# Norms by matmul, denominators kept in SBUF, a new chunk order and operand loads by threes in a hybrid encoder layer

## The chip, the cores and the metric

The kernel runs on one core of a Trainium2 chip. The metric is the device time of one execution in microseconds. Three runs of the kernel before took 1853.64, 1854.88 and 1856.46 us; the median, 1854.88 us, is the time that the change is compared with.

## The reference, cut to what matters

One encoder layer is applied to a prompt of 1024 tokens and to a sample of 512 tokens with the same weights. Model width is 1024, the FFN's hidden width 2816, everything in float32.

```
h    = rms_norm(x) * (1 + sc1) + sh1
proj = h @ w_in                       # q, k, v of 12 heads; u, v of 4 gMLP groups
o_g, lse_g = dilated_window_attention(q, k, v) for 3 groups of 4 heads
wts  = softmax(lse over the 3 groups)
mix  = concat(wts_g * o_g, u * (W_s LN(v) + b)) @ w_out
x    = x + gt1 * rms_norm(mix)
h    = rms_norm(x) * (1 + sc2) + sh2
f    = (silu(gate) * up) @ w_down,  gate, up = split(h @ w_gu)
y    = x + gt2 * rms_norm(f)
```

The weighting of the three attention groups by their log-sum-exps is done in the kernel as one division: the unnormalised outputs of the groups are multiplied by the reciprocal of the sum of their denominators. A head's slot (0 or 1) says which half of the four heads of a group it belongs to, and each slot has its own denominators.

## The kernel before, in words

The activations lie with features on the 128 partitions, in chunks of 128 features by 512 tokens, eight chunks for the model width (`KC`). The prompt is two halves of 512 tokens (group 0 and group 1, together the class `P`), the sample is group 2 (class `S`). Every product is done as three matmuls of float32r operands, high by high, high by low and low by high (`mm3`, L160). For that, `split` (L139) makes the high part of an operand with a cast on ACT (L140) and the low part with a subtraction on DVE or POOL (L141). Weights come from DRAM by one DMA queue that SP issues in order (four raw buffers `wraw`), are split, and are used from `whl`; chunks come through `load_chunk` (L237) into three buffers `xc`.

The stages are: input projections and attention of the sample and then the prompt, gMLP of the two prompt halves, out-projections of groups 2, 0 and 1 (`out_proj`, `post`), the FFN of the sample (`ffn`, `down`), and the FFN of the prompt, whose first product over both halves is a Winograd product with seven products instead of eight (`operands` writes 28 operand chunks to `ops` in DRAM, `operands_in` loads and splits them, `ffn_up` multiplies), and last `ffn_down` for the halves 0 and 1.

Work that is not the matmuls of the running stage is written as generators. They are queued in `self.back`, and each product calls `tick`, which lets them go on; `alongside` starts one beside the running stage. After that a scheduling pass orders the instructions of each engine, so that the order on an engine is not that of the code.

The places that the change touches: `attention_slot` (L713) takes the reciprocal of a slot's denominators (L729) and writes them to `rden` in DRAM (L731); `mix_in` (L902) loads each of the eight chunks of the attention and gMLP output, loads the denominators again for each of the six attention chunks, multiplies (L907) and splits with the low part on POOL. `post` (L831) evacuates an out-projection tile into an `sc` buffer (L843), squares it (L844), and when the norm is there multiplies by it (L856), adds the residual (L857) and stores. The norm is either `rms` (L202: a matmul with ones sums over the partitions, POOL takes the power, ACT makes a diagonal tile and matmuls with ones spread it over the partitions) or, after the FFN of groups 2 and 0, `rms_slow` (L195):

```
self.nc.gpsimd.partition_all_reduce(ss, ss, channels=128, reduce_op=RED.add)
y = self.t("rs", [128, 512])
self.rsqrt(y, self.t2("tb"), self.t2("tb"), ss, 1.0 / D, RMS_EPS)
```

where `rsqrt` (L170) is twelve DVE operations on 128x512 tiles, nine of them in the loop L179 to L181, with two of the two `tb` buffers. `ffn_up` makes the combined weights on DVE (L929, L986), and evacuates products into `tb` on ACT (L1036).

Of the kernel before, what the change touches and what calls it, by code (L numbers as in the profile page):

```python
# [10 lines left out]
F32R = mybir.dt.float32r  # L11
I32 = mybir.dt.int32
# [7 lines left out]
D = 1024  # L20
KC = 8
# [9 lines left out]
RSQRT_MAGIC = 0x5F3759DF  # L31
# [47 lines left out]
class Layer:  # L79
    def __init__(self, tc, ctx, a):  # L80
# [16 lines left out]
        self.rs2 = {}  # L97
        self.pending = []
# [71 lines left out]
    def rsqrt(self, y, v, t, ss, scale, eps):  # L170

        nc = self.nc
        nc.vector.tensor_scalar(out=v, in0=ss, scalar1=scale, scalar2=eps, op0=ALU.mult, op1=ALU.add)
        nc.vector.tensor_scalar(out=y.bitcast(I32), in0=v.bitcast(I32), scalar1=1, scalar2=None,
                                op0=ALU.arith_shift_right)
        nc.vector.tensor_scalar(out=y.bitcast(I32), in0=y.bitcast(I32), scalar1=-1, scalar2=RSQRT_MAGIC,
                                op0=ALU.mult, op1=ALU.add)
        for _ in range(3):
            nc.vector.tensor_tensor(out=t, in0=y, in1=y, op=ALU.mult)  # L179
            nc.vector.scalar_tensor_tensor(out=t, in0=v, scalar=-0.5, in1=t, op0=ALU.mult, op1=ALU.mult)  # L180
            nc.vector.scalar_tensor_tensor(out=y, in0=t, scalar=1.5, in1=y, op0=ALU.add, op1=ALU.mult)  # L181

# [11 lines left out]

    def rms_slow(self, ss):  # L195

        self.nc.gpsimd.partition_all_reduce(ss, ss, channels=128, reduce_op=RED.add)  # L197
        y = self.t("rs", [128, 512])
        self.rsqrt(y, self.t2("tb"), self.t2("tb"), ss, 1.0 / D, RMS_EPS)
        return y  # L200
# [512 lines left out]
    def attention_slot(self, grp, sp, steps, between=None, start=None):  # L713
# [9 lines left out]
        def behind():  # L723
            while len(vs) < 3:
                yield
            yield from weave(self.softmax(grp, sc[0]), self.softmax(grp, sc[1]))
            den = self.t4("st")
            yield from self.values(grp, sp, sc, vs, den)
            self.nc.vector.reciprocal(out=den[:, :grp.n], in_=den[:, :grp.n])  # L729
            for hf, gi in enumerate(grp.halves):  # L730
                self.nc.sync.dma_start(out=self.rden[gi, sp], in_=den[:, 512 * hf:512 * hf + 512])  # L731
            yield
# [98 lines left out]
    def post(self, gi, product, G, xsrc, dst, follow, steps):  # L831
# [32 lines left out]
        def behind():  # L864
            rs = self.rms(ss) if follow else self.rms_slow(ss)
# [36 lines left out]
    def mix_in(self, gi, hs, kcs=range(KC), tags=("h",) * KC):  # L902
        for kc in kcs:
            x = self.load_chunk(self.mix[gi, kc])
            if kc < 6:
                r = self.load_chunk(self.rden[gi, kc % 2])
                self.nc.vector.tensor_tensor(out=x, in0=x, in1=r, op=ALU.mult)  # L907
            h = self.t(tags[kc], [128, 2, 512], F32R)
            self.split(h[:, 0], h[:, 1], x, self.nc.gpsimd)
            hs.append(h)  # L910
            yield

    def out_proj(self, gi, hs, steps):
        def product(mt):
            w = self.weights(self.a["wout"][mt], share=SHARE[3])
            ps = self.p("mm")
            self.mm3(ps, w, range(KC), hs)
# [46 lines left out]
    def operands_in(self, ops, os):  # L964
        for o in os:
            for k in range(4):
                x = self.load_chunk(self.ops[o, k])
                h = self.t(self.OPS[4 * o + k], [128, 2, 512], F32R)
                self.split(h[:, 0], h[:, 1], x)
                ops[o].append(h)  # L970
                yield
# [101 lines left out]
    def ffn(self, gi, h2, ops):  # L1073
# [19 lines left out]
        self.back.append(self.operands_in(ops, range(2)))  # L1093
# [23 lines left out]
    def run(self):  # L1117
# [55 lines left out]
        self.back.append(self.mix_in(0, hs[0]))  # L1173
# [8 lines left out]
        self.back.insert(0, self.ffn_in(2, h2))  # L1182
# [10 lines left out]
        for _ in self.operands_in(ops, range(2, 7)):  # L1193
            pass
# [10 lines left out]
STEPS = (3, 6, 3, 4)  # L1205
H0 = 'V'
H1 = 'V'
H2 = 'V'
H3 = 'P'
# [60 lines left out]
```

## Time and profile before

| what | value |
|---|---|
| median of three runs | 1854.88 us (1853.64 to 1856.46) |
| the profiled execution's own time | 1856.45 us |
| span of its records | 1854.7 us |
| mean granted clock of TensorE | 0.986 |
| TensorE (PE) busy | 1785.3 us, 96% |
| VectorE (DVE) busy | 1049.6 us, 57% |
| ScalarE (ACT) busy | 694.3 us, 37% |
| GpSimd (POOL) busy | 113.3 us, 6% |

Busy time counts instructions that run, not those that wait. The span is the time from the first record to the last of one execution; its own time lies 1.75 us above it. Where the stages lie in the span: the first out-projection tile is evacuated (L843) at 574.6 us, the first tile of the sample's FFN (L1086) at 759.0 us, the first and the last product of the Winograd FFN (L1036) at 1146.5 and 1571.4 us; what comes after are the down products of the prompt.

### The profile page before, as it was taken

What the parts mean: (1) busy time and instruction counts of PE and PEld (TensorE: products, weight loads), DVE (VectorE), ACT (ScalarE), POOL (GpSimd) and SP (SyncE); (2) the same over time, 40 slices, a digit from 0 to 9 for tenths busy, and PEclk for the clock granted to TensorE, in tenths of its full rate; (3) what the DMA queues carried; (4) which work ended last, traced back from release to release, by engine and by line L of the source; (5) the groups of instructions that cost most, each with busy time, mean ns of one, the idle gap of its engine ahead of it and who ended that gap; (6) DMA issues with size and microseconds to landing.
All of it is one profiled execution on the core that took longest, in us unless ns stands there. A gap on an engine that the chain in (4) does not pass through costs nothing.

```text
span 1854.7 us, 22895 instructions
## 1 busy us (share of the span) xinstructions
PE 1785.3 (96%) x8442; PEld 1402.8 (76%) x8442; DVE 1049.6 (57%) x1675; ACT 694.3 (37%) x1196; POOL 113.3 (6%) x70
## 2 busy tenths in 40 slices
PE   6999999999999889899999998799999999999997
PEld 3787777766787667677888886588888888888886
DVE  4686625524876556766444325766666576623733
ACT  4653511411355346444333324233232233533322
POOL 0010100300121132000000000000000000000001
PEclk9999999999999999899999998899999999999998
DMA  8424312211243465568422435332222222734632
GB/s 323 148 95 161 130 63 98 80 68 63 93 144 114 146 215 194 185 233 299 143 94 94 135 97 161 112 123 80 92 80 86 80 91 73 238 98 157 216 106 77
DMA packets 133617, 245.05 MB, mean 132 GB/s; under 512 B 14976, under 2 KB 20352, under 8 KB 133504
## 3 DMA queue, kind: packets, MB, share of 16 engines
q1 hardware_dynamic: 133360, 243.51, 39.5%
q8 instruction: 66, 1.08, 0.2%
q14 instruction: 47, 0.39, 0.1%
q10 hardware_dynamic: 144, 0.07, 0.0%
HBM read 204.20 MB, written 39.32 MB: 131 GB/s over the span
## 4 chain that ended last, share of the span: by engine, by line
PE 84%; issue 5%; DVE 5%; DMA 3%; ACT 1%; POOL 1%; SPq 0%; DVEq 0%; ACTq 0%; POOLq 0%
PE pmm L158 69%; PE ppv L158 9%; PE pst L158 6%; DMA xc<-rden 1%; DVE sc L618 1%; POOL st L653 1%; DMA xc<-ops 1%; DVE whl L141 1%; DMA xc<-in_x 0%; DVE sc L856 0%; DMA h<-in_wada 0%; POOL h L141 0%; DMA xc<-mix 0%; DVE sd L618 0%; ACT tb L389 0%
## 5 line engine op out<-in xcount | busy, mean ns | idle before, releaser
L158 PE MATMUL pmm<-h,whl 128*128 128x512 f32 x4008 | 990.4, 401 | 32.6 <-ACT whl L140 11.2
L158 PEld LDWEIGHTS pmm<-h,whl 128*128 128x128 f32 x4008 | 749.8, 190 | 241.6 <-issue 28.7
L141 DVE TENSOR_TENSOR whl<-wraw,whl 128x512 fp32r<-128x512 f32 (+1 forms) x420 | 290.4, 695 | 317.7 <-ACT whl L140 317.6
L140 ACT CAST whl<-wraw 128x512 fp32r<-128x512 f32 (+1 forms) x420 | 253.2, 606 | 469.7 <-PE pmm L158 342.6
L158 PE MATMUL pmm<-qk,whl 128*128 128x512 f32 (+1 forms) x570 | 141.1, 394 | 0.0
L158 PEld LDWEIGHTS pmm<-qk,whl 128*128 128x128 f32 x570 | 107.1, 188 | 25.3 <-DVE whl L141 0.3
L158 PE MATMUL pmm<-v,whl 128*128 128x512 f32 x405 | 102.6, 398 | 10.7 <-ACT tb L1036 10.7
L158 PE MATMUL pmm<-h,sc 128*128 128x512 f32 x408 | 101.0, 395 | 0.0
L158 PEld LDWEIGHTS pmm<-v,whl 128*128 128x128 f32 x405 | 77.5, 192 | 28.6 <-ACT tb L1036 11.1
L158 PEld LDWEIGHTS pmm<-h,sc 128*128 128x128 f32 x408 | 76.7, 188 | 18.3
L158 PE MATMUL pst<-qk 64*128 64x128 f32 (+3 forms) x384 | 66.9, 319 | 0.9 <-DVE qk L141 0.9
L140 ACT CAST whl<-sd 128x512 fp32r<-128x512 f32 x53 | 32.9, 620 | 87.9 <-PE ppv L158 69.1
L158 PE MATMUL ppv<-h,whl 128*128 128x512 f32 x264 | 65.1, 395 | 0.0
L158 PEld LDWEIGHTS pst<-qk 64*128 64x128 f32 (+1 forms) x384 | 49.2, 187 | 20.6 <-issue 12.9
L197 POOL PARTITION_ALL_REDUCE acc<-acc x2 | 7.0, 3514 | 895.7 <-issue 568.8
L158 PEld LDWEIGHTS ppv<-h,whl 128*128 128x128 f32 x264 | 49.6, 188 | 11.9
L140 ACT CAST h<-xc 128x512 fp32r<-128x512 f32 x56 | 34.5, 621 | 54.7 <-DVE xc L907 29.9
L653 POOL PARTITION_ALL_REDUCE st<-st x8 | 34.6, 4326 | 317.1 <-DVE st L589 289.2
L192 DVE TENSOR_TENSOR acc<-acc,ta 128x512 f32<-128x512 f32 x48 | 33.1, 689 | 36.2 <-ACT ta L844 31.5
L141 DVE TENSOR_TENSOR whl<-sd,whl 128x512 fp32r<-128x512 f32 x53 | 36.5, 689 | 28.9 <-ACT whl L140 28.8
L843 ACT ACTIVATE sc<-pmm,G 128x512 f32<-128x512 f32 x47 | 32.3, 688 | 43.9 <-PE pmm L158 40.1
L493 DVE SCALAR_TENSOR_TENSOR sc<-cst,pst 128x512 f32<-128x512 f32 (+2 forms) x56 | 27.0, 512 | 36.7 <-PE pst L158 31.7
(206 smaller groups left out, 1948.0 us busy)
## 6 DMA issues: line engine op xcount, KB each, us to landing
wraw<-in_wgu SPq DMA_DIRECT2D x132, 256.0 KB, 2.8
wraw<-in_wdn SPq DMA_DIRECT2D x120, 256.0 KB, 2.6
wraw<-in_win SPq DMA_DIRECT2D x80, 256.0 KB, 2.7
xc<-in_x SPq DMA_DIRECT2D x56, 256.0 KB, 3.3
xc<-in_wada SPq DMA_DIRECT2D x48, 256.0 KB, 3.6
wraw<-in_wout SPq DMA_DIRECT2D x48, 256.0 KB, 3.1
sd<-in_wgu SPq DMA_DIRECT2D x44, 256.0 KB, 3.3
xc<-hid SPq DMA_DIRECT2D x44, 256.0 KB, 3.2
```

Of the source, the lines that this page charges most:

```text
L140: self.nc.scalar.copy(hi, src)
L141: (eng or self.nc.vector).tensor_tensor(out=lo, in0=src, in1=hi.bitcast(F32), op=ALU.subtract)
L158: self.nc.tensor.matmul(out, lhsT, rhs, start=start, stop=stop, skip_group_check=True)
L192: nc.vector.tensor_tensor(out=acc, in0=acc, in1=t, op=ALU.add)
L197: self.nc.gpsimd.partition_all_reduce(ss, ss, channels=128, reduce_op=RED.add)
L493: self.nc.vector.scalar_tensor_tensor(out=out, in0=table, scalar=slope, in1=ps, op0=ALU.mult, op1=ALU.add)
L618: nc.vector.tensor_tensor(out=o, in0=o, in1=m, op=ALU.subtract)
L653: self.nc.gpsimd.partition_all_reduce(x[:, :grp.n], x[:, :grp.n], channels=128, reduce_op=RED.max)
L843: nc.scalar.activation(ys[-1][:, mt % 2], ps, AF.Copy, scale=G[:, mt, c:c + 1])
```

## The change

All norms go through `rms`; `rms_slow` and `rsqrt` are gone. The reciprocal is taken for each half by itself, and for slot 1 of the prompt the result stays in SBUF (`self.den`) instead of going to `rden`. `mix_in` loads the denominators of a slot once into an `rs` buffer, takes the chunks of prompt groups in the order `MIXED`, in which the chunks of slot 1 (1, 3, 5) come last, and makes the low parts on DVE. Twelve of the twenty late operands (numbers 8 to 19) are loaded three at a time into `sd` buffers of 128x3x512. `mix_in(0)` is started with `alongside`, the sample's `ffn_in` is queued last instead of first, and splits its chunks on DVE (`H3`).

```diff
@@ attention_slot
-            self.nc.vector.reciprocal(out=den[:, :grp.n], in_=den[:, :grp.n])
             for hf, gi in enumerate(grp.halves):
-                self.nc.sync.dma_start(out=self.rden[gi, sp], in_=den[:, 512 * hf:512 * hf + 512])
-            yield
+                d = den[:, 512 * hf:512 * hf + 512]
+                self.nc.vector.reciprocal(out=d, in_=d)
+                if grp is self.P and sp:
+                    self.den[gi] = d
+                else:
+                    self.nc.sync.dma_start(out=self.rden[gi, sp], in_=d)
+                yield
@@ post
-            rs = self.rms(ss) if follow else self.rms_slow(ss)
+            rs = self.rms(ss)
@@ mix_in
-    def mix_in(self, gi, hs, kcs=range(KC), tags=("h",) * KC):
-        for kc in kcs:
+    def mix_in(self, gi, hs):
+        r = {}
+        for sp in range(1 if gi < 2 else 2):
+            r[sp] = self.load_chunk(self.rden[gi, sp], "rs")
+        for kc in self.mixed(gi):
             x = self.load_chunk(self.mix[gi, kc])
             if kc < 6:
-                r = self.load_chunk(self.rden[gi, kc % 2])
-                self.nc.vector.tensor_tensor(out=x, in0=x, in1=r, op=ALU.mult)
-            h = self.t(tags[kc], [128, 2, 512], F32R)
-            self.split(h[:, 0], h[:, 1], x, self.nc.gpsimd)
+                while kc % 2 not in r:
+                    if gi in self.den:
+                        r[1] = self.den[gi]
+                    else:
+                        yield
+                self.nc.vector.tensor_tensor(out=x, in0=x, in1=r[kc % 2], op=ALU.mult)
+            h = self.t("h", [128, 2, 512], F32R)
+            self.split(h[:, 0], h[:, 1], x)
@@ out_proj
-            self.mm3(ps, w, range(KC), hs)
+            self.mm3(ps, w, self.mixed(gi), hs)
@@ operands_in(self, ops, first, last, wide)
+        src = self.ops.rearrange("o k p t -> p (o k) t")
+        i = first
+        while i < last:
+            if i < first + wide:
+                n = min(3, first + wide - i)
+                t = self.t("sd", [128, 3, 512])
+                self.nc.sync.dma_start(out=t[:, :n], in_=src[:, i:i + n])
+                xs = [t[:, j] for j in range(n)]
+            else:
+                xs = [self.load_chunk(src[:, i])]
...
@@ run
-        self.back.append(self.mix_in(0, hs[0]))
+        self.alongside(self.mix_in(0, hs[0]))
...
-        self.back.insert(0, self.ffn_in(2, h2))
+        self.back.append(self.ffn_in(2, h2))
...
-        for _ in self.operands_in(ops, range(2, 7)):
+        for _ in self.operands_in(ops, 8, 28, 12):
...
+MIXED = (6, 7, 0, 2, 4, 1, 3, 5)
-H3 = 'P'
+H3 = 'V'
```

Line numbers move with the edit: what L856, L907 and L141 are before is L839, L898 and L140 in the changed kernel, and the reciprocal L729 is L710. The scheduling pass orders the new kernel anew, so three places of the order are shown.

The first is DVE between the last denominators of prompt slot 1 (`st`) and the out-projection of prompt half 0. Before, in the order of the engine:

```order
L729 RECIPROCAL st<-st 128x1024
L141 TENSOR_TENSOR whl<-wraw,whl 128x512
L192 TENSOR_TENSOR acc<-acc,ta 128x512
L141 TENSOR_TENSOR whl<-wraw,whl 128x512 x2
L192 TENSOR_TENSOR acc<-acc,ta 128x512
L141 TENSOR_TENSOR whl<-wraw,whl 128x512
L907 TENSOR_TENSOR xc<-xc 128x512
L217 TENSOR_SCALAR rq<-pst 128x4
L907 TENSOR_TENSOR xc<-xc 128x512 x2
L856 TENSOR_TENSOR sc<-sc,rs 128x512 x8
L907 TENSOR_TENSOR xc<-xc 128x512
```

The same place in the changed kernel:

```order
L687 TENSOR_TENSOR st<-st,ppv 128x4x128 x2
L710 RECIPROCAL st<-st 128x512 x2
L196 TENSOR_SCALAR rq<-pst 128x4
L898 TENSOR_TENSOR xc<-xc,st 128x512 x3
L140 TENSOR_TENSOR h<-xc,h 128x512 x5
L898 TENSOR_TENSOR xc<-xc,rs 128x512
L839 TENSOR_TENSOR sc<-sc,rs 128x512 x3
L898 TENSOR_TENSOR xc<-xc,rs 128x512
L839 TENSOR_TENSOR sc<-sc,rs 128x512 x5
L140 TENSOR_TENSOR h<-xc,h 128x512
L140 TENSOR_TENSOR whl<-wraw,whl 128x512
L898 TENSOR_TENSOR xc<-xc,rs 128x512
```

The products with the denominators now read `st` in SBUF and follow the two reciprocals at once; the low parts of operand chunks (`h<-xc,h`) are new on DVE, and eight products with the sample's norm (L839) and splits stand ahead of the next weight's low part.

The second is SP's queue at the change from the sample's FFN to the Winograd product (`in_wdn` and `in_wgu` are the weights, `ops` the operands). Before:

```order
L150 DMA wraw<-in_wdn 128x256
L1031 DMA wraw<-in_wgu 128x512 x2
L239 DMA xc<-ops 128x512 x3
L1031 DMA wraw<-in_wgu 128x512
L239 DMA xc<-ops 128x512
L1031 DMA wraw<-in_wgu 128x512
L239 DMA xc<-ops 128x512 x11
L1031 DMA wraw<-in_wgu 128x512 x2
L239 DMA xc<-ops 128x512 x2
```

The same place in the changed kernel:

```order
L149 DMA wraw<-in_wdn 128x256
L1035 DMA wraw<-in_wgu 128x512 x2
L966 DMA sd<-ops 128x3x512
L1035 DMA wraw<-in_wgu 128x512
L966 DMA sd<-ops 128x3x512
L1035 DMA wraw<-in_wgu 128x512
L1035 DMA sd<-in_wgu 128x512 x3
L218 DMA xc<-ops 128x512 x2
L1035 DMA sd<-in_wgu 128x512
L218 DMA xc<-ops 128x512 x3
```

Two of the four wide loads stand here; the other two stand right behind the last operand's store, ahead of the sample's FFN weights. The remaining single loads are split into three of the earlier down product and five here.

The third is the norm of the sample's FFN, in the second unit of the Winograd product. Before, on DVE:

```order
L179 TENSOR_TENSOR tb<-rs 128x512
L929 TENSOR_TENSOR sd<-sd 128x512
L180 SCALAR_TENSOR_TENSOR tb<-tb 128x512
L986 TENSOR_TENSOR sd<-sd 128x512
L181 SCALAR_TENSOR_TENSOR rs<-tb,rs 128x512
L179 TENSOR_TENSOR tb<-rs 128x512
L180 SCALAR_TENSOR_TENSOR tb<-tb 128x512
L181 SCALAR_TENSOR_TENSOR rs<-tb,rs 128x512
L179 TENSOR_TENSOR tb<-rs 128x512
L180 SCALAR_TENSOR_TENSOR tb<-tb 128x512
L181 SCALAR_TENSOR_TENSOR rs<-tb,rs 128x512
```

In the changed kernel, on PE, in the first unit:

```order
L157 MATMUL pmm<-h,whl 128x512 x36
L157 MATMUL pst<-ones,acc 128x2 x4
L157 MATMUL pmm<-h,whl 128x512 x2
L157 MATMUL pmm<-v,whl 128x512 x2
L157 MATMUL pmm<-h,whl 128x512 x10
L157 MATMUL pmm<-v,whl 128x512 x7
L157 MATMUL pmm<-qk,whl 128x512 x3
L157 MATMUL ppv<-qk,whl 128x512 x3
L157 MATMUL ppv<-vm,whl 128x512 x6
L157 MATMUL ppv<-sc,whl 128x512 x3
L157 MATMUL pst<-tb,ones 128x128
L157 MATMUL pmm<-qk,whl 128x512 x12
```

The sum over the partitions (`pst<-ones,acc`) and the spread (`pst<-tb,ones`) now stand between products of the first unit; the operations L173 to L181 are on no engine.

## Rows read from the trace of the kernel before

**Rows 1.** The page's first part: busy time, share of the span, instructions of each engine.

```profile
PE 1785.3 (96%) x8442; PEld 1402.8 (76%) x8442; DVE 1049.6 (57%) x1675; ACT 694.3 (37%) x1196; POOL 113.3 (6%) x70
```

**Rows 2.** Busy time by stretch: stretch, its length, engines, granted clock, DMA share, GB/s.

```profile
620.00:680.00 60.00, 48.70 (x196) 37.40 (x195) 33.29 (x40) 23.62 (x44) 17.97 (x14) 0.94 0.56 180
680.00:730.00 50.00, 48.46 (x221) 39.02 (x220) 33.18 (x48) 33.47 (x60) 14.09 (x11) 1.00 0.67 221
1195.00:1840.00 645.00, 644.29 (x2840) 523.25 (x2840) 379.05 (x596) 212.89 (x374) 4.27 (x2) 1.00 0.36 116
```

**Rows 3.** Timeline of PE: start, duration, work, then idle before it and releaser.

```profile
750.37 14.87 PE L158 MATMUL pmm<-h,whl 128*128 128x512 f32 x51 [9.56 <-ACT ta L844]
...
1149.86 1.22 PE L158 MATMUL pmm<-h,whl 128*128 128x512 f32 x2 [8.04 <-ACT whl L140]
...
1188.65 4.21 PE L158 MATMUL pmm<-v,whl 128*128 128x512 f32 x9 [10.71 <-ACT tb L1036]
...
1197.80 2.36 PE L158 MATMUL pmm<-h,whl 128*128 128x512 f32 x9 [0.71 <-DVE whl L141]
```

**Rows 4.** Busy time by stretch, columns as in rows 2: after PE's gaps.

```profile
633.00:637.00 4.00, 3.79 (x14) 3.39 (x14) 0.69 (x1) 1.76 (x6) 2.25 (x2) 0.57 0.57 172
664.00:667.50 3.50, 3.49 (x9) 2.70 (x10) 2.39 (x3) 2.41 (x5) 1.27 (x1) 0.54 0.74 221
743.00:756.00 13.00, 5.63 (x13) 4.45 (x14) 9.85 (x16) 6.83 (x12) 0.00 (x0) 0.50 0.71 237
1145.00:1156.00 11.00, 6.14 (x15) 4.84 (x16) 10.80 (x16) 5.67 (x11) 3.50 (x1) 0.53 0.53 169
1183.00:1193.00 10.00, 4.35 (x10) 3.47 (x11) 9.80 (x17) 0.58 (x1) 0.00 (x0) 0.50 0.01 2
```

**Rows 5.** Waits from 610 to 700 us: engine, releaser, sum, times, longest.

```profile
ACT h L140 <- DVE xc L907: 24.2, 10, 3.6
DVE xc L907 <- DMA xc<-rden: 19.6, 10, 3.2
```

**Rows 6.** Groups of instructions, 618 to 700 us: busy and mean ns, then idle before.

```profile
L141 POOL TENSOR_TENSOR h<-xc,h 128x512 fp32r<-128x512 f32 x15 | 21.1, 1411 | 30.4 <-ACT h L140 24.9 <-issue 5.4
L140 ACT CAST h<-xc 128x512 fp32r<-128x512 f32 x15 | 9.3, 622 | 27.3 <-DVE xc L907 24.2 <-DMA xc<-mix 3.2
```

**Rows 7.** Timeline of DVE: last denominators of prompt slot 1, their reciprocal.

```profile
615.96 1.24 DVE L708 TENSOR_TENSOR st<-st,ppv 128x512 f32<-128x512 f32 x1 [3.69 <-PE ppv L158]
...
618.29 6.55 DVE L729 RECIPROCAL st<-st 128x1024 f32<-128x1024 f32 x1
```

**Rows 8.** DMA issues, 610 to 700 us: count, size, median us to landing.

```profile
xc<-mix SPq DMA_DIRECT2D x14, 256.0 KB, 2.9
xc<-rden SPq DMA_DIRECT2D x11, 256.0 KB, 2.7
...
rden<-st SPq DMA_DIRECT2D x2, 256.0 KB, 2.3
```

**Rows 9.** Waits from 735 to 760 us, columns as in rows 5.

```profile
ACT sc L843 <- DMA x<-sc: 2.6, 1, 2.6
```

**Rows 10.** Chain of work that ended last, 1138 to 1192 us: start, us, what.

```profile
1132.66 5.45 DMA xc<-ops
...
1146.37 2.74 DVE wraw L929
```

**Rows 11.** Timeline of POOL: the all-reduce of the sample's norm.

```profile
1146.07 3.50 POOL L197 PARTITION_ALL_REDUCE acc<-acc  x1 [326.86 <-DVE acc L192]
```

**Rows 12.** Timeline of DVE, 1176 to 1192 us.

```profile
1181.86 0.69 DVE L929 TENSOR_TENSOR sd<-sd 128x512 f32<-128x512 f32 x1
...
1189.24 3.09 DVE L856 TENSOR_TENSOR sc<-sc,rs 128x512 f32<-128x512 f32 x5
```

**Rows 13.** Timeline of ACT, 1176 to 1192 us.

```profile
1188.02 0.58 ACT L1036 COPY tb<-pmm 128x512 f32<-128x512 f32 x1 [9.41 <-DVE tb L180]
```

**Rows 14.** Timeline of PE: the spread of one norm at full clock.

```profile
737.42 1.05 PE L158 MATMUL pst<-tb,ones 128*128 128x128 f32 x8
```

More of the change, by code (lines that the diff above doesn't have):

```diff
@@ L11 @@
 F32R = mybir.dt.float32r
-I32 = mybir.dt.int32
 AF = mybir.ActivationFunctionType
@@ L30 @@
 GELU_A = 0.044715
-RSQRT_MAGIC = 0x5F3759DF
 def alibi(h):
@@ L97, in __init__ @@
         self.rs2 = {}
+        self.den = {}
         self.pending = []
@@ L168, in mm3 @@
             self.mm(out, wl, hk[:, 0], False, last and i == n - 1)
[L170 to L181, printed above, removed]
     def square_sum(self, squares):
@@ L193, in square_sum @@
         return acc
[L195 to L200, printed above, removed]
     def rms(self, ss, keep=True):
@@ L900, in post_last, with mixed @@
                 nc.sync.dma_start(out=dst[:, 2 * j:2 * j + 2, o], in_=y)
-    def mix_in(self, gi, hs, kcs=range(KC), tags=("h",) * KC):
-        for kc in kcs:
+    def mix_in(self, gi, hs):
[3 more added lines that the diff above has]
+        for kc in self.mixed(gi):
             x = self.load_chunk(self.mix[gi, kc])
             if kc < 6:
-                r = self.load_chunk(self.rden[gi, kc % 2])
-                self.nc.vector.tensor_tensor(out=x, in0=x, in1=r, op=ALU.mult)
-            h = self.t(tags[kc], [128, 2, 512], F32R)
-            self.split(h[:, 0], h[:, 1], x, self.nc.gpsimd)
+                while kc % 2 not in r:
[6 more added lines that the diff above has]
+            self.split(h[:, 0], h[:, 1], x)
             hs.append(h)
             yield
+    def mixed(self, gi):
+        return range(KC) if gi == 2 else MIXED
     def out_proj(self, gi, hs, steps):
@@ L962, in operands, with operands_in @@
             yield
[L964 to L968, printed above, removed]
+    def operands_in(self, ops, first, last, wide):
+        src = self.ops.rearrange("o k p t -> p (o k) t")
[8 more added lines that the diff above has]
+                xs = [self.load_chunk(src[:, i])]
+            for x in xs:
+                h = self.t(self.OPS[i], [128, 2, 512], F32R)
                 self.split(h[:, 0], h[:, 1], x)
-                ops[o].append(h)
+                ops[i // 4].append(h)
+                i += 1
                 yield
@@ L1092, in ffn @@
             self.tick(2)
-        self.back.append(self.operands_in(ops, range(2)))
+        self.back.append(self.operands_in(ops, 0, 8, 0))
         self.down(gi, hid)
```

## The prediction

> **What bounds the kernel now.** I read the engine totals first: TensorE (PE) is busy 1785.3 of the 1854.7 us span, every other engine 57% or less [rows 1]. So time can only come from PE's gaps, 69.4 us in all, or from work added to or taken off PE. Next, PE by stretches: the long one from 1195 to 1840 us has 0.7 us of gap, whereas 620 to 680 us loses 11.30 and 680 to 730 us 1.54 [rows 2]. The timeline of PE gives the other large gaps: 9.56 us before 750.37, 8.04 before 1149.86, 10.71 before 1188.65 and 0.71 before 1197.80 [rows 3]. Behind each gap PE runs for a while at a granted clock near half (1.2 instead of 2.4 GHz) [rows 4]; I price that as busy time x (1 - clock).
>
> That makes four places:
> - **A, out-projection of the sample into that of prompt half 0:** 12.84 + 3.79 x 0.43 + 3.49 x 0.46 = 16.1 us. The waits there run in a chain: the product with the denominators waits for their loads, 19.6 us in 10 waits, and ACT's cast waits 24.2 us for that product [rows 5]. Those loads come after a reciprocal of 6.55 us and a write to DRAM [rows 7, 8].
> - **B, start of the sample's FFN:** 9.56 + 5.63 x 0.50 = 12.4 us. PE waited for ACT's evacuation of an out-projection tile [rows 3], and ACT for an sc buffer (a store out of sc) [rows 9], freed late because the norm of prompt half 0 came late.
> - **C1, start of the Winograd FFN:** 8.04 + 6.14 x 0.47 = 10.9 us. The first weights wait in DVE's queue behind operand splits that wait for single loads; the chain shows 5.45 us of such a load, and one weight combination of 2.74 us, which ran while POOL's all-reduce did, against 0.69 elsewhere [rows 10 to 12].
> - **C2, its second unit:** 10.71 + 0.71 + 4.35 x 0.50 = 13.6 us. ACT could not evacuate to a tb tile before the reciprocal square root of the sample's norm had let its tb tiles go: the copy idled 9.41 us [rows 13].
>
> Sum 53.0 us. The rest of the gaps lies at the two ends and is not touched.
>
> **The change part by part.** The sum is made on the profiled execution, 1856.45 us, which is 1.57 above the median of 1854.88. Without the four places: 1856.45 - 53.0 = 1803.4.
>
> *All norms on TensorE.* Two norms leave POOL and DVE. PE gains, for each, eight short matmuls for the sum and eight for the spread; a spread spans 1.05 us, and I take the sum, with its shorter matmuls, as no longer [rows 14]. 4 x 1.05 = 4.2 us, all on the bound engine. The second norm's old form (prompt half 0, in the last stretch but the end) cost PE nothing [rows 2], so it pays without return. Removed with them are 9 DVE operations per norm, about 0.69 each, and 3.5 us of POOL [rows 11, 12]. For C2 this is the whole cure: the eight products L839 (L856 before) now stand as a block in DVE's order, 8 x 0.61 = 4.9 us, but the spread that they wait for is issued a whole product ahead. I leave 1 us. (0.61 is the spacing of such products: 3.09 us for five [rows 12].)
> The Trainium skill speaks against this part: "GPSIMD Engine Reference", section Engine selection, gives reductions along the partition dimension to GpSimd, and "Perfetto Trace Analysis", section Identifying Performance Opportunities, says that what counts is the most-contended engine, which here is PE. By those alone the part costs 4.2 us and returns nothing. The trace disagrees in C2: PE's largest gap there ends on the norm that GpSimd's reduction feeds.
>
> *Denominators in SBUF, slot-1 chunks last.* Take X as the end of the last denominator matmul of prompt slot 1. Before, after X came 1.24 of addition, 6.55 of reciprocal [rows 7], a write of 2.3 and loads of 2.7 us [rows 8]. Now: two additions overlap to X+1.4, two reciprocals of half the width run one after the other, 6.55 together, to X+8.0; product 0.69 and cast 0.62 [rows 6] follow to X+9.4. PE has only 13 matmuls of 0.23 left after X (644.29 us for 2840 [rows 2]), 3.0 us, and stands 6 us. The next weights' low parts are behind a block in DVE's order: five operand splits, two products with rs whose chunk loads could start only when the three xc buffers came free (2.9 us a load [rows 8]), eight L839 of 0.61 and one more split: the second low part is done at about X+24.4. PE reaches that weight at about X+17, since its 18 matmuls between run at half clock, and stands another 7.3. Clock loss 3.5 + 1.5 = 5. Together 18.3, take 18: no gain over the 16.1. Splits that went from POOL (1.41 each [rows 6]) to DVE (0.69) are in these orders.
>
> *In B,* the norm of prompt half 0 now stands early in the next out-projection, so its sc buffers come free and the 9.56 goes. New: the sample's FFN input is queued last instead of first, so its spread is at the end of the last out-projection. From the order I read 1.9 us while the h2 chunks form and 3.1 us where DVE's next eight products (4.9 us) stand before a weight's low part, with 1.7 of clock: 6.7.
>
> *In C1,* 12 operands come by threes: two wide loads long ahead, two just before the first Winograd weights, eight single ones after. Six DVE operations (about 4 us) remain before the first low parts; PE stands 2.8 and loses 1 to the clock: 3.8. The trace has no 768 KB load: below, it takes no longer than a 256 KB one (2.9), above, three in a row (8.7). I take neither as binding, because two of the four land a stage early; if the later two took 8.7, C1 would be 3 us worse.
> The Trainium skill ("DMA: Bandwidth & Descriptors", section Anatomy of one DMA) gives 2.0 us plus the bytes at 436 GB/s, an estimate of 3.8 us; by it C1 stays as it is.
>
> **Sum:** 1803.4 + 4.2 + 18 + 6.7 + 3.8 + 1 = 1837.1, less 1.57: 1835.5, say **1836 us**, 19 below the median.
>
> **The rivals.**
> 1. *A is cured too* (24%). If the eight L839 do not hold up the weights, only the first wait (6 us and 1.5 of clock) is left: 10.5 less, 1825. For it: the rden loads, on which DVE waited 19.6 us [rows 5], are mostly gone from PE's path. Against: the block stands in the order.
> 2. *Weights late behind chunk loads* (15%). On SP's queue the chunk loads of prompt half 1 stand ahead of weight loads and wait for xc buffers. If six go one after the other, 2.9 + 0.69 + 0.62 + 0.69 = 4.9 each, the weight comes at X+9.4+29.4+4.2 = X+43, PE is out of work at X+32, and A grows by 11: 1847.
> 3. *The same, slower than before* (3%). If no two of the eight chunk chains ahead of the third pair of weights overlap, 39 us pass: the weight comes at X+53, PE stands 21 more and loses 3 of clock: 1860. The point where the sign turns is about seven chains in a row. Against it: before, chunk and denominator loads overlapped.
> 4. *The gaps only move* (4%). C2's wait was the last of several; if the next one (operands, weights) ends as late in each place, only the 4.2 us of PE work stays: 1859. This is what the skill's rule above gives if the trace misleads me. Against: B's and C2's releasers [rows 9, 13] are gone from the order altogether.
>
> **How the numbers follow.** My case has 54%, with its own range of 1829 to 1843 (A 13 to 23, C1 up to 3 more, B 2 either way). A measurement of this kernel tells some 0.2%, 3.7 us, from no change. My case, the first rival and the second are faster: 0.90 with some taken off for mixtures of the second and third. Rivals 3 and 4 sit near the edge or beyond it: slower 0.05, within 0.2% 0.05. The range takes in the first rival with a little more in B and C1, and the second: 1819 to 1850.
>
> **What would show it.** Right: no wait of ACT for L180's tb tiles (C2), none of ACT for sc buffers (B); a gap of PE near 6 us after the last denominators and a second one of 5 to 9 us ending on a weight's low part, behind L839; C1 under 4 us; PE busy time up by about 4 less the half-clock time. Wrong: A under 10 us (rival 1), a PE gap that ends on a weight's DMA around the second third of the out-projection of half 0 (rivals 2, 3), or new gaps in the stretches that were full before.

## The result, and the profile after

The changed kernel takes 1832.49 us (median of four runs, 1831.16 to 1834.55), the kernel before 1854.34 us in the same measurement: a ratio of 0.9881, 95% interval 0.9864 to 0.9898, so 21.9 us or 1.2% less. The profiled execution took 1831.72 us with a span of 1830.0 us, 24.7 us under the span before.

PE is the first thing to read again. Its busy time on the page, and its busy time by stretch (columns as in rows 2):

```profile
PE 1782.8 (97%) x8474; PEld 1405.2 (77%) x8474; DVE 1036.8 (57%) x1687; ACT 696.5 (38%) x1206; POOL 62.9 (3%) x38
```

```profile
620.00:700.00 80.00, 67.24 (x326) 53.72 (x325) 53.38 (x77) 36.60 (x66) 2.39 (x3) 0.89 0.51 168
700.00:780.00 80.00, 77.19 (x342) 61.55 (x342) 59.16 (x97) 48.97 (x90) 3.38 (x3) 0.98 0.60 203
1120.00:1160.00 40.00, 36.45 (x153) 29.38 (x152) 30.09 (x51) 18.51 (x35) 1.48 (x1) 0.91 0.46 162
1160.00:1200.00 40.00, 39.84 (x172) 31.94 (x172) 30.49 (x49) 11.79 (x20) 0.00 (x0) 1.00 0.54 176
```

PE runs 32 more matmuls [rows 1], which are the two norms, and yet is busy 2.5 us less. That goes with the mean granted clock, 0.989 against 0.986 before: less of PE's work stands behind a gap and runs near half clock. The gaps in the four stretches sum to 12.76 + 2.81 + 3.55 + 0.16 = 19.3 us. Before they were 11.30 + 1.54 [rows 2] in A and 9.56, 8.04, 10.71 and 0.71 [rows 3] in B, C1 and C2, 41.9 us together. So 22.6 us of the 24.7 are gaps that closed; the rest, some 2 us, is shorter busy time. The largest gaps that are left in PE's timeline (start, duration, work, then idle before it and releaser):

```profile
639.69 1.22 PE L157 MATMUL pmm<-h,whl 128*128 128x512 f32 x2 [5.61 <-ACT h L139]
...
648.52 0.73 PE L157 MATMUL pmm<-h,whl 128*128 128x512 f32 x2 [1.61 <-ACT whl L139]
651.68 1.22 PE L157 MATMUL pmm<-h,whl 128*128 128x512 f32 x2 [2.43 <-ACT whl L139]
654.66 19.38 PE L157 MATMUL pmm<-h,whl 128*128 128x512 f32 x70 [1.76 <-DVE whl L140]
675.39 10.27 PE L157 MATMUL pmm<-h,whl 128*128 128x512 f32 x43 [1.35 <-DVE whl L140]
...
766.34 0.90 PE L157 MATMUL pmm<-h,whl 128*128 128x512 f32 x2 [2.26 <-ACT acc L843]
...
1132.19 1.02 PE L157 MATMUL pst<-ones,acc 128*128 128x2 f32 x8 [0.62 <-DVE acc L178]
1136.15 1.22 PE L157 MATMUL pmm<-h,whl 128*128 128x512 f32 x2 [2.93 <-ACT whl L139]
```

The reader is to see three things. C2's wait on ACT's copy into tb [rows 13] is gone. B's 9.56 us is gone, and a small one of 2.26 us stands 16 us later in its place. A is as large as before, in two parts: 5.61 us that ends on the cast of the first slot-1 chunk, and then 7.15 us in four pieces on weights, of which two (4.04 us) end on ACT's cast of a weight and two (3.11 us) on DVE's low part of one.

What those low parts wait for stands in DVE's timeline (start, duration, work):

```profile
631.80 6.57 DVE L710 RECIPROCAL st<-st 128x512 f32<-128x512 f32 x2
...
646.70 1.89 DVE L839 TENSOR_TENSOR sc<-sc,rs 128x512 f32<-128x512 f32 x3
...
649.11 3.09 DVE L839 TENSOR_TENSOR sc<-sc,rs 128x512 f32<-128x512 f32 x5
...
652.72 0.68 DVE L140 TENSOR_TENSOR whl<-wraw,whl 128x512 fp32r<-128x512 f32 x1
...
653.92 1.28 DVE L140 TENSOR_TENSOR whl<-wraw,whl 128x512 fp32r<-128x512 f32 x2
...
674.04 0.69 DVE L840 TENSOR_TENSOR sc<-sc,xc 128x512 f32<-128x512 f32 x1 [0.72 <-DMA xc<-in_x]
...
760.09 4.91 DVE L839 TENSOR_TENSOR sc<-sc,rs 128x512 f32<-128x512 f32 x8 [4.05 <-ACT rs L213]
```

The two reciprocals take 6.57 us in a row, about as one of double width did (6.55) [rows 7]. The eight products L839 end at 652.2, with one operand split and the next weight's low part behind them; the second low part, begun at 653.92, lets PE go on at 654.66. The fourth piece, 1.35 us before 675.39, has another cause: its low part stands behind a residual addition (L840), and that waited for a load of x. The 2.26 us before 766.34, at the sample's FFN, stand behind the next block of eight products, at 760.09.

### The profile page after: what moved, and what is told of

It is laid out like the page before. It is cut to its first block, busy times and chain, and to the rows that moved or that the text cites. A ratio compares the mean times of both kernels' runs of the same rounds, so it can differ in the third digit from the quotient of the medians.

```text
span 1830.0 us, 22847 instructions
## 1 busy us (share of the span) xinstructions
PE 1782.8 (97%) x8474; PEld 1405.2 (77%) x8474; DVE 1036.8 (57%) x1687; ACT 696.5 (38%) x1206; POOL 62.9 (3%) x38
## 4 chain that ended last, share of the span: by engine, by line
PE 88%; DVE 5%; DMA 3%; issue 1%; ACT 1%; POOL 1%; SPq 0%; DVEq 0%; ACTq 0%
PE pmm L157 72%; PE ppv L157 10%; PE pst L157 6%; DMA xc<-hid 1%; DVE sc L597 1%; POOL st L632 1%; DVE sc L839 1%; DVE whl L140 1%; DMA xc<-mix 1%; DMA xc<-in_x 0%; DMA h<-in_wada 0%; DVE st L710 0%; DVE sd L597 0%; DVE h L140 0%; DVE sc L840 0%
## 5 line engine op out<-in xcount | busy, mean ns | idle before, releaser
L140 DVE TENSOR_TENSOR whl<-wraw,whl 128x512 fp32r<-128x512 f32 (+1 forms) x420 | 281.5, 674 | 330.8 <-ACT whl L139 330.4
L157 PEld LDWEIGHTS pmm<-qk,whl 128*128 128x128 f32 x570 | 106.7, 188 | 24.7
L157 PEld LDWEIGHTS pmm<-v,whl 128*128 128x128 f32 x405 | 76.4, 189 | 17.4
L197 POOL TENSOR_TENSOR rq<-rq,half 128x4 f32<-128x4 f32 (+1 forms) x13 | 14.4, 1109 | 1344.7 <-DVE rq L196 1017.8
L157 PEld LDWEIGHTS ppv<-h,whl 128*128 128x128 f32 x264 | 49.7, 188 | 11.8
L140 DVE TENSOR_TENSOR whl<-sd,whl 128x512 fp32r<-128x512 f32 x53 | 36.5, 689 | 26.3 <-ACT whl L139 26.2
L1018 DVE TENSOR_TENSOR st<-st,ppv 128x512 f32<-128x512 f32 x44 | 30.2, 685 | 26.8 <-PE ppv L157 26.4
L140 DVE TENSOR_TENSOR h<-xc,h 128x512 fp32r<-128x512 f32 x56 | 37.8, 687 | 13.0 <-ACT h L139 12.7
```

What stands on the lines that cost most here:

```text
L140: (eng or self.nc.vector).tensor_tensor(out=lo, in0=src, in1=hi.bitcast(F32), op=ALU.subtract)
L157: self.nc.tensor.matmul(out, lhsT, rhs, start=start, stop=stop, skip_group_check=True)
L197: nc.gpsimd.tensor_tensor(out=y, in0=y, in1=self.half8[:, :n], op=ALU.pow)
L1018: add = lambda o, a, b: nc.vector.tensor_tensor(out=o, in0=a, in1=b, op=ALU.add)
```

## The experiments

Ratios are to the kernel before, measured beside the run in question; the changed kernel has 0.9881 (0.9864 to 0.9898). Two ratios closer than some 0.003 are not told apart by their intervals, so the gaps of the profile carry the verdict there.

**The norms undone.** `post` takes the old form again behind the two down products:

```diff
-            rs = self.rms(ss)
+            rs = self.rms(ss) if follow else self.rms_slow(ss)
```

> The changed kernel with one part undone: the two norms behind the down products go back to the all-reduce on POOL and the reciprocal square root on DVE. Theory (the norm's old form held the tb tiles that the second Winograd unit needs, C2): PE idles 9 to 12 us again before a pmm<-v product in the second unit, on ACT's copy into tb, some 2 us of clock go with it, and about 4 us of PE work go away; 1839 to 1843 us. Rival (the gaps only move, what counts is PE's own work): no gap over 3 us comes back there, and the time falls by up to 4 us, to 1828 to 1832.

0.9931 (0.9916 to 0.9946), 1843.6 us. Timeline of PE at the start of the Winograd product and in its second unit, of ACT in that unit, of POOL and of DVE at the start of the product:

```profile
1136.79 1.22 PE L159 MATMUL pmm<-h,whl 128*128 128x512 f32 x2 [6.57 <-ACT whl L141]
...
1174.77 4.08 PE L159 MATMUL pmm<-v,whl 128*128 128x512 f32 x9 [10.69 <-ACT tb L1062]
```

```profile
1174.13 0.58 ACT L1062 COPY tb<-pmm 128x512 f32<-128x512 f32 x1 [9.40 <-DVE tb L181]
```

```profile
1131.17 3.51 POOL L198 PARTITION_ALL_REDUCE acc<-acc  x1 [323.31 <-DMA xc<-ops]
```

```profile
1130.89 0.68 DVE L1012 TENSOR_TENSOR wraw<-wraw 128x512 f32<-128x512 f32 x1
1131.49 2.73 DVE L1012 TENSOR_TENSOR sd<-sd 128x512 f32<-128x512 f32 x1
```

PE's gap in the second unit is back with 10.69 us and the same releaser as before [rows 13]. The gaps at the start of the product grew from 3.55 us (0.62 and 2.93) to 6.57: one weight combination again takes 2.73 us while the all-reduce runs, against 0.68 just ahead. So the old form cost two places, not one: the theory held for C2, and part of C1 belongs to it as well. How much of C1's part is that one slow combination, and how much the rest of the old form, was not tried apart.

**The norms alone,** in the kernel before: the same line, in the other direction.

```diff
-            rs = self.rms(ss) if follow else self.rms_slow(ss)
+            rs = self.rms(ss)
```

> The kernel before with one part of the change done alone: its last norms go through the matmul form too. Theory (the norms' old form made C2's gap and part of C1's, and nothing else): C2's gap of 10.7 us goes, C1's falls from 8 to 4 to 6 us, A and B stay as before; about 11 us less than the kernel before, a ratio of 0.993 to 0.995. Rival (the norms help only together with the other parts): under 6 us less, 0.997 or more.

0.9925 (0.9909 to 0.9941). PE's timeline around the starts of the sample's FFN and of the Winograd product:

```profile
752.63 16.43 PE L158 MATMUL pmm<-h,whl 128*128 128x512 f32 x59 [9.90 <-ACT ta L844]
```

```profile
1146.60 1.35 PE L158 MATMUL pst<-ones,acc 128*128 128x2 f32 x8 [3.09 <-DVE acc L192]
1149.12 1.22 PE L158 MATMUL pmm<-h,whl 128*128 128x512 f32 x2 [1.18 <-ACT whl L140]
1184.41 5.38 PE L158 MATMUL pmm<-h,whl 128*128 128x512 f32 x22 [0.82 <-DVE whl L141]
```

C1 is down from 8.04 to 4.27 us and C2 from 11.42 to 0.82, while B's gap stays (9.90); A's gaps, expected to stay too, are 14.7 us instead of 12.8. About 14 of the 22 us come from the norms alone, against some 11 that were expected; PE's own extra work is in that figure.

**Single operand loads.** No operand by threes:

```diff
-        for _ in self.operands_in(ops, 8, 28, 12):
+        for _ in self.operands_in(ops, 8, 28, 0):
```

> The changed kernel with one part undone: all twenty late operands are loaded singly into xc buffers. Theory (C1 was a matter of the operand loads in front of the first Winograd weights): PE idles 8 us or more at the start of the Winograd product instead of 3.6, with 1 to 2 us more at half clock; 1837 to 1841 us. Rival (C1 went because the all-reduce and the square root left DVE and POOL): the gap stays at 3 to 5 us, and the time at 1831 to 1834 us.

0.9882 (0.9866 to 0.9898), no difference that this can tell. PE's timeline at the start of the product:

```profile
1132.64 1.02 PE L157 MATMUL pst<-ones,acc 128*128 128x2 f32 x8 [3.15 <-DVE acc L178]
1135.26 1.22 PE L157 MATMUL pmm<-h,whl 128*128 128x512 f32 x2 [1.59 <-ACT whl L139]
```

4.74 us of gap against 3.55: the rival held. The wide loads are worth 1.2 us of gap; the rest of C1's gain is the norms'.

**The denominators through DRAM again,** loaded once for each half; chunk order and low parts as changed:

```diff
                 self.nc.vector.reciprocal(out=d, in_=d)
+                self.nc.sync.dma_start(out=self.rden[gi, sp], in_=d)
                 if grp is self.P and sp:
-                    self.den[gi] = d
-                else:
-                    self.nc.sync.dma_start(out=self.rden[gi, sp], in_=d)
+                    self.den[gi] = True
...
-                        r[1] = self.den[gi]
+                        r[1] = self.load_chunk(self.rden[gi, 1], "rs")
```

> The changed kernel with one part undone: the denominators of prompt slot 1 go through DRAM again, loaded once for a half; the chunk order stays. Theory (the first gap of A is the chain from the last denominators to the first slot-1 chunk): that gap grows from 5.6 by the write and the load, 2.3 and 2.7 us, to 10 to 11 us; what follows it in DVE's order is less pressed, so the sum over A grows by 2 to 5 us; 1834 to 1838 us. Rival (A is set by the weights' low parts behind other DVE work, however early the denominators are): the sum over A stays within 2 us; 1831 to 1834 us.

0.9844 (0.9827 to 0.9860): faster than the changed kernel, which neither side had expected. PE's timeline and DVE's:

```profile
636.74 1.22 PE L157 MATMUL pst<-tb,ones 128*128 128x128 f32 x4 [5.89 <-ACT tb L208]
...
647.15 0.72 PE L157 MATMUL pmm<-h,whl 128*128 128x512 f32 x2 [1.92 <-ACT whl L139]
649.30 13.02 PE L157 MATMUL pmm<-h,whl 128*128 128x512 f32 x48 [1.43 <-DVE whl L140]
663.62 22.11 PE L157 MATMUL pmm<-h,whl 128*128 128x512 f32 x94 [1.30 <-ACT whl L139]
```

```profile
646.73 0.68 DVE L140 TENSOR_TENSOR whl<-wraw,whl 128x512 fp32r<-128x512 f32 x1
...
655.08 4.90 DVE L838 TENSOR_TENSOR sc<-sc,rs 128x512 f32<-128x512 f32 x8
```

The round trip cost the products only 1.52 us of wait on DVE, not 5; the first gap, 5.89 us, ends on the norm's diagonal tile and not on a chunk. The scheduling pass put the eight products (here L838) behind several low parts instead of ahead of them. A's gaps fell to 10.5 us. A new theory: it is the place of this block in DVE's order that decides A, not how the denominators travel.

**The block held back.** That theory was tried in the changed kernel, denominators in SBUF, by a dependence that changes no value:

```diff
+            if gi == 2 and follow:
+                while len(self.wl0) < 3:
+                    yield
+                lo = self.wl0[2][1][:, 1, 0:1].bitcast(F32)
+                nc.vector.scalar_tensor_tensor(out=rs[:, 0:1], in0=lo, scalar=0.0, in1=rs[:, 0:1],
+                                               op0=ALU.mult, op1=ALU.add)
             fs = [fin(mt, rs) for mt in range(KC)]
```

(`wl0` collects the weights of the out-projection of half 0.)

> The changed kernel with an artificial dependence: the sample's norm waits for the low part of the third weight of the next out-projection (a one-column operation that adds zero), so that the eight products L839 stand behind two weights' low parts in DVE's order instead of ahead of them; the denominators stay in SBUF. Theory (in A the block costs the second wait, and a run of the kernel with the denominators through DRAM was faster since its order put the block later): the gaps of A after the first one fall from 7.1 us together to 4 to 5, with less time at half clock; 3 to 6 us faster than the changed kernel, a ratio to the kernel before of 0.985 to 0.987. Rival (the run through DRAM was faster by some other way): 0.988 as the changed kernel, or slower.

0.9834 (0.9818 to 0.9849), 1827.0 us. PE's gaps in A:

```profile
639.53 1.22 PE L158 MATMUL pmm<-h,whl 128*128 128x512 f32 x2 [5.61 <-ACT h L140]
648.46 0.74 PE L158 MATMUL pmm<-h,whl 128*128 128x512 f32 x2 [2.00 <-ACT whl L140]
650.45 8.66 PE L158 MATMUL pmm<-h,whl 128*128 128x512 f32 x24 [1.25 <-DVE whl L141]
660.42 27.69 PE L158 MATMUL pmm<-h,whl 128*128 128x512 f32 x118 [1.31 <-ACT whl L140]
```

The first gap is untouched, those behind it fell from 7.15 to 4.56 us, and the one of 2.26 us at the sample's FFN to 0.74. So the block explains 2.6 us of A; two of the three pieces that are left end on ACT's cast of a weight. By the ratios the gain against the changed kernel is some 8 us, more than the 3 to 6 expected; the gaps account for 4.5 us of it (2.6 in A, 1.9 in B), and the spans of the two profiled executions differ by 4.0. The kernel is not told apart from the one with denominators in DRAM. The gap at the sample's FFN shrank to 0.7 or 0.8 us in all four kernels of this section that are below 0.9855; why was not tried.

**The second reciprocal held back,** behind the three products of half 0, by a similar one-column operation:

```diff
-                self.nc.vector.reciprocal(out=d, in_=d)
                 if grp is self.P and sp:
+                    if hf == 0:
+                        self.nc.vector.reciprocal(out=d, in_=d)
                     self.den[gi] = d
...
+                if gi == 0 and kc == KCL:
+                    d = self.den[1]
+                    self.nc.vector.scalar_tensor_tensor(out=d[:, 0:1], in0=x[:, 0:1], scalar=0.0, in1=d[:, 0:1],
+                                                        op0=ALU.mult, op1=ALU.add)
+                    self.nc.vector.reciprocal(out=d, in_=d)
```

(`KCL` is 5, the last slot-1 chunk.)

> The changed kernel with the reciprocal of prompt half 1 held behind the three products of half 0 (a one-column operation that adds zero makes the dependence). Theory (PE's first gap in A is the chain of two reciprocals in a row): the gap falls from 5.6 by one reciprocal of 3.3 us to 2 to 2.6, and the time by 2 to 4 us if the gaps behind it stay, a ratio of 0.986 to 0.987. Rival (the later weights are the limit, so the time comes back in the next gap): the gaps of A keep their sum of 12 to 13 us, 0.988.

0.9855 (0.9838 to 0.9871). PE's first gap in A:

```profile
636.13 1.22 PE L157 MATMUL pmm<-h,whl 128*128 128x512 f32 x2 [2.51 <-ACT h L139]
```

The first gap fell from 5.61 to 2.51 us, as the theory says; the gaps behind it then add up to 9.3 us instead of 7.15, so A keeps 11.8 of 12.8 us. By the gaps the rival held for the most part: the later weights took back most of what the first gap gave. The time lies at the theory's 0.986, but is not told apart from the changed kernel's.

**Both held back.** The two edits together:

> The changed kernel with both artificial dependences: the second reciprocal behind the three products of half 0, and the sample's norm behind the third weight's low part. Theory (two separate waits in A, so the gains add): A's gaps fall to 6 to 8 us in all, and the time by 2 to 4 us against the run with the held norm alone, a ratio of 0.981 to 0.983. Rival (with the block out of the way the first gap is made up for later or the operand loads become the limit): within 1 us of that run, 0.983 to 0.985.

0.9825 (0.9809 to 0.9842), 1824.8 us (1820.3 to 1825.2), with gaps of PE of 7.5 us in all of A. The gaps add as the theory says; the time against the run with the held norm alone is not told apart by the intervals. It beats both kernels: 32 us or 1.75% under the kernel before.

**Plain chunk order,** 0 to 7, a chunk loaded when its denominators are known. The load moves behind the wait because chunk 1 would otherwise be loaded before slot 1's outputs are in DRAM, so two things differ from the changed kernel:

```diff
-            x = self.load_chunk(self.mix[gi, kc])
             if kc < 6:
                 while kc % 2 not in r:
...
+            x = self.load_chunk(self.mix[gi, kc])
+            if kc < 6:
...
-MIXED = (6, 7, 0, 2, 4, 1, 3, 5)
+MIXED = (0, 1, 2, 3, 4, 5, 6, 7)
```

> The changed kernel with one part undone: prompt chunks in the order 0 to 7, each loaded after its denominators are known, so that chunks 2 to 7 of half 0 wait behind chunk 1 and with it for slot 1. Theory (the order takes five of eight chunks out of the chain from the last denominators): the gaps of A together grow from 12.8 us by 4 to 9, and the time as much, a ratio of 0.990 to 0.993. Rival (A's sum is set by the weights behind DVE's block, however late the chunks are): within 3 us of the changed kernel, 0.987 to 0.990.

0.9851 (0.9835 to 0.9868), again not slower. PE's timeline:

```profile
637.20 8.71 PE L157 MATMUL pmm<-h,whl 128*128 128x512 f32 x28 [7.79 <-ACT h L139]
648.29 11.14 PE L157 MATMUL pmm<-h,whl 128*128 128x512 f32 x40 [2.38 <-DVE h L140]
660.24 30.02 PE L157 MATMUL pmm<-h,whl 128*128 128x512 f32 x128 [0.81 <-DVE whl L140]
```

The first gap grew by 2.2 us only, and the next ones are smaller. DVE's block of eight products ran from 642.7 to 647.6 us here, mostly while PE still had the work that it finished at 645.9; the second gap, 2.38 us, ends on an operand's low part right behind the block. A's sum is 11.0 us. The time lies below what either side had asked for; the order by itself has no gain here.

**Low parts of the chunks on POOL again:**

```diff
-            self.split(h[:, 0], h[:, 1], x)
+            self.split(h[:, 0], h[:, 1], x, self.nc.gpsimd)
```

> The changed kernel with one part undone: the low parts of the attention and gMLP chunks go back to POOL. Theory (DVE's queue sets A's second wait): five low parts leave DVE ahead of the weight, 3 us, while POOL's take 1.4 instead of 0.7 us each, in A's first gap too; the gaps of A keep their sum within 2 us, and the time is within 3 us of the changed kernel, 0.987 to 0.990. Rival (POOL's low parts are what A's chunk chains wait for): A's gaps grow by 4 us or more, 0.990 to 0.993.

0.9914 (0.9899 to 0.9929), 6 us slower than the changed kernel: the rival held. Timelines of POOL and of DVE in A:

```profile
651.72 1.61 POOL L140 TENSOR_TENSOR h<-xc,h 128x512 fp32r<-128x512 f32 x1 [1.27 <-ACT h L139]
```

```profile
650.91 5.98 DVE L839 TENSOR_TENSOR sc<-sc,rs 128x512 f32<-128x512 f32 x8
```

The block takes 5.98 instead of 4.90 us with that one subtraction of POOL beside it, and just ahead DVE waits 6.59 us for a chunk load; that the xc buffers are held longer by POOL is the likely reason, not a shown one. PE's gaps from 620 to 700 us are 17.4 against 12.8 us. The Trainium skill ("SBUF — State Buffer", section Who interferes with whom) says that a DVE instruction with two SBUF inputs contends with a GpSimd instruction that reads SBUF; these rows and the 2.73 us above agree with it.

**B: the queue of the sample's FFN input.** Queued first again:

```diff
-        self.back.append(self.ffn_in(2, h2))
+        self.back.insert(0, self.ffn_in(2, h2))
```

> The changed kernel with one part undone: the sample's FFN input is queued first again instead of last. Theory (B went because the norm of prompt half 0 is no longer queued behind the sample's FFN input): the wait of ACT for sc buffers and a gap of 8 to 10 us at the start of the sample's FFN come back, with 2 to 3 us of clock, while the small gap of 2.3 us there now goes; 1839 to 1843 us. Rival (B went because the out-projections' DVE and POOL work got shorter): no gap over 3 us comes back; 1829 to 1833 us.

0.9888 (0.9873 to 0.9903). PE's timeline, the spread of half 0's norm and the gap:

```profile
727.87 1.05 PE L157 MATMUL pst<-tb,ones 128*128 128x128 f32 x8
...
744.03 20.18 PE L157 MATMUL pmm<-h,whl 128*128 128x512 f32 x79 [2.31 <-ACT ta L827]
```

The gap that came back is 2.31 us on ACT's evacuation at 744 us, not 8 to 10; the 2.26 us gap behind it went. ACT's wait for an sc buffer did come back, with 4.6 us. The rival held: no gap over 3 us.

**The same with its low parts on POOL** (`H3 = 'P'`):

> The changed kernel with two parts undone: the sample's FFN input queued first again, and its chunks' low parts back on POOL. Theory (B's gap is the diagonal tile of prompt half 0's norm, which stands behind the eight FFN-input chunks in the tb tiles; POOL's slower low parts stretch that stream): against the run with the first part alone, the stream of chunks gets some 6 us longer, the norm's spread that much later, and the gap on ACT's evacuation of an out-projection tile grows from 2.3 to 7 to 9 us; 5 to 8 us more than that run, a ratio of 0.992 to 0.994. Rival (what shortened B there was the denominator part): the gap stays at 2 to 4 us, 0.988 to 0.990.

0.9861 (0.9847 to 0.9876): the theory fell. The gap from 700 to 780 us is 0.37 us, below the rival's 2 to 4 as well, and POOL's low parts did not stretch the stream by 6 us. Timelines of PE, the sum of the sample's second norm in this run, and in the changed kernel that sum and the spread of half 0's norm:

```profile
686.52 0.95 PE L157 MATMUL pst<-ones,acc 128*128 128x2 f32 x8
```

```profile
685.50 0.95 PE L157 MATMUL pst<-ones,acc 128*128 128x2 f32 x8
...
705.85 1.05 PE L157 MATMUL pst<-tb,ones 128*128 128x128 f32 x8
```

In the kernel before the sum stood at

```profile
705.29 1.02 PE L158 MATMUL pst<-ones,acc 128*128 128x2 f32 x8
```

and the spread of half 0's norm at 737.42 [rows 14]. So the sample's second norm is ready 19 us earlier with the changed chunk code, its FFN-input chunks pass through the tb tiles earlier, and half 0's norm behind them is spread 10 us earlier (727.87 with the queue order of before) and frees its sc buffers nearly in time. With the sample's FFN input queued last the spread comes another 22 us earlier, at 705.85. Why this run has 0.37 us of gap and the one before it 2.31 stays open.

**The whole chunk and denominator part undone,** norms, wide loads and queue order kept:

```diff
-        self.alongside(self.mix_in(0, hs[0]))
+        self.back.append(self.mix_in(0, hs[0]))
...
-    def mix_in(self, gi, hs):
+    def mix_in(self, gi, hs, kcs=range(KC), tags=("h",) * KC):
...
+                r = self.load_chunk(self.rden[gi, kc % 2])
...
+            self.split(h[:, 0], h[:, 1], x, self.nc.gpsimd)
...
```

> The changed kernel with the whole denominator part undone: one reciprocal for both halves, written to DRAM, denominators loaded for each chunk, low parts of the chunks on POOL, chunks in order, the old start of the first chunks. Norms, wide loads, and the order of the sample's FFN input stay as changed. Theory (A gains nothing from this part, and B goes by the queue order and the norm): A's gaps 12 to 13 us as in both, B without a gap over 3 us; within 3 us of the changed kernel, 0.987 to 0.990. Rival (fewer loads and DVE instead of POOL are what cured B): a gap of 6 to 10 us at B on ACT's evacuation of an out-projection tile, 0.992 to 0.996.

0.9910 (0.9892 to 0.9928), some 5 us more than the changed kernel, which the intervals hardly tell apart. A's gaps are 13.0 us from 620 to 700, as in both kernels; half 0's norm is spread at 718.57, earlier than in the kernel before; from 700 to 780 us the gaps are 7.0 us, in pieces of which the largest waits for DVE's sum of squares (L853):

```profile
718.57 1.05 PE L157 MATMUL pst<-tb,ones 128*128 128x128 f32 x8
...
747.07 0.58 PE L157 MATMUL pst<-ones,acc 128*128 128x2 f32 x4 [2.58 <-DVE acc L853]
```

So with the old chunk code the queue order takes the 9.56 us away and leaves most of the loss in other places, and with the new chunk code no gap over 3 us is left in B whatever the queue order. Each side was partly right.

## Why the prediction was right, point by point

The forecast was 1836 us in a range of 1819 to 1850; it came to 1832.5. By its terms, gaps and clock loss (busy time times one minus the granted clock) of the changed kernel:

| term | forecast | measured |
|---|---|---|
| A | 18 | 12.76 + 3.9 = 16.7 |
| B | 6.7 | 2.81 + 1.5 = 4.3 |
| C1 | 3.8 | 3.55 + 2.5 = 6.0 |
| C2 | 1 | 0.16 |
| norms on PE | 4.2 | 3.2 |

The clock losses are worked out from these stretches (columns as in rows 2), the first two for A, then B and C1:

```profile
639.00:648.00 9.00, 7.22 (x26) 5.73 (x26) 6.38 (x11) 5.84 (x13) 0.85 (x1) 0.73 0.48 139
648.00:658.00 10.00, 5.29 (x12) 3.49 (x13) 10.00 (x17) 5.11 (x10) 0.00 (x0) 0.63 0.37 116
...
762.00:778.00 16.00, 13.53 (x51) 10.20 (x51) 15.13 (x26) 8.07 (x15) 0.00 (x0) 0.89 0.66 225
1132.00:1144.00 12.00, 8.88 (x30) 7.24 (x31) 9.46 (x17) 6.47 (x14) 1.48 (x1) 0.72 0.51 168
```

The norms' 3.2 us are an estimate: four times 0.81 us, the time from the start of an unbroken series of eight matmuls, the spread at 1712.54 us in the changed kernel, to the next matmul's start. Of the other three series two are interleaved with products, and one, at 1132.19 us, fell among C1's gaps and spans 1.02 us. Put into the forecast's sum, these terms give 1803.4 + 16.7 + 4.3 + 6.0 + 0.2 + 3.2 = 1833.8, 2 us above the profiled execution's 1831.72.

- *A without a gain* was right: 16.7 us against 16.1 before and 18 forecast. The first gap was right in size and reason, 6 us against 5.61, the two reciprocals in a row; holding the second one back shows it. The wait behind it was right in its end: the second low part at X+24.4, with X near 630.5 us (the last addition starts there), is 654.9, and PE went on at 654.66. That 7.3 and 7.15 us agree is in part luck. The three pieces up to that low part are 5.80 us; the fourth, 1.35, comes 20 us later behind a load of x and is no term of the forecast. Nor is the block L839 the whole reason: held back, it leaves 4.56 of the 7.15 us, most of it on ACT's casts. Rival 1 had everything but the first gap go with the block; the run in which the block is out of the way does not show that.
- *C2* was right in cause and size; the undone norms bring the same wait back.
- *C1* was near in its gap (3.55 us against 2.8), low on the clock (2.5 against 1) and wrong in cause. The step that failed is the one that gave C1 to the loads by threes: those are worth 1.2 us of gap (single loads: 4.74 against 3.55), and the norms take the gap from 8.04 to 4.27 by themselves. The row that told it was read, a weight combination of 2.74 us beside the all-reduce [rows 10, 11], but given no share in the sum. The wide loads took a median of 5.5 us to landing, between the forecast's bounds of 2.9 and 8.7 and above its estimate of 3.8 from the Trainium skill, whose section gives its figure for DMAs on the gpsimd path, while these go through SP's queue.
- *B* was right in its mechanism, incomplete in its cause and 2.4 us too high. As forecast, half 0's norm is spread early (705.85 us instead of 737.42), the 9.56 us are gone, and a gap stands where DVE's next eight products are ahead of a weight's low part: 2.26 us and 0.21 behind it, 3.1 forecast. The 1.9 us while the h2 chunks form came to 0.21. What the forecast left out is that the new chunk code does the larger part of the cure: it gets the sample's second norm through 19 us earlier, and with it alone, the queue order undone, 2.3 us of gap are left (0.4 with POOL's low parts), while the queue order with the old chunk code leaves 7.0. Which piece of the chunk code does that, one load of the denominators per slot or the earlier start of the chunks, was not tried apart. The engine of the low parts, the chunk order and the denominators' place, each undone alone, leave that norm's sum at 692.9, 690.1 and 685.6 us, so none of them is needed for it.
- *The rule against the norms* (cross-partition sums to GpSimd, since PE is the contended engine), which was made rival 4, would have given 1859 us. The runs decide against it here: the two norms cost PE some 3.2 us, and the kernels with and without them differ by 9 (undone) to 14 us (alone) in their favour.
- *Rivals 2 and 3* (weights behind chunk loads on SP's queue) did not show: the gaps of A end on casts and low parts of weights, none on a weight's load.

Two parts of the change did not do what they look meant for: keeping the denominators in SBUF and taking the slot-1 chunks last. Each, undone alone, gave a kernel at 0.984 to 0.985. That is most likely a matter of the order that the scheduling pass then writes on DVE: the held norm, with denominators in SBUF and the new order of chunks, has 0.9834.

## What to carry to other kernels

Where one engine is busy 96% of the time, price a change by the few gaps of that engine and by what ends each one; here 22.6 of the 24.7 us gained came out of four places. Then test each term by itself, since a sum can come out right with a cause wrong, as C1 did. A data path made shorter gains nothing if the engine that consumes it runs a block of unrelated work ahead of what the bound engine needs next: look at that engine's order, and move the block by a dependence before moving data. A small reduction kept off the bound engine can cost it more than the same sum done there: here the kernels with the all-reduce and the twelve DVE operations behind it are 9 to 14 us slower, though they spare PE some 3 us of matmuls.

## What the runs showed of the hardware

A 128x512 operation with two SBUF inputs on DVE took 2.73 us, four times its 0.68, beside the all-reduce on POOL (3.5 us), in the kernel before and in the one with the norms undone; with one subtraction on POOL beside them eight products took 5.98 us instead of 4.90. A round trip of the denominators through DRAM, a write and a load that took 2.3 and 2.7 us to landing in the kernel before [rows 8], left DVE only 1.52 us of wait: the write of the first half was issued at 632.0 us, while the second half's reciprocal ran until 635.2. Two reciprocals of 128x512 took as long (6.57 us) as one of 128x1024 (6.55).
